# JS divergence on one core: four fp32 first loads made by both hardware queues in halves, with new ranges and orders

## Chip, cores and metric

The kernel runs on one core of a Trainium2 chip. The metric is the device time of one execution in microseconds (us).

## The reference

```python
batch, dim = 1024, 4096            # p, q: fp32, rows sum to 1
def reference(p, q):
    m = 0.5 * (p + q)
    kl_pm = np.sum(p * np.log(p / (m + 1e-8) + 1e-8), axis=-1)
    kl_qm = np.sum(q * np.log(q / (m + 1e-8) + 1e-8), axis=-1)
    return (0.5 * (kl_pm + kl_qm)).astype(np.float32)
```

Each output is a sum over one row of 4096 columns.

## The kernel before

The 1024 rows are 8 row groups (g0 to g7) of 128 rows, one row per partition. Each group is cut along its columns into ranges, and there are four different cuts: `LOADS` (what one load brings), `LOGS` (what one logarithm of p and q covers), `PRODUCTS` (the buffers `ab` that hold these logarithms) and `SUMS` (the ranges of s = p + q and of its logarithm c). Ranges are numbered through all groups. Every quantity is a logarithm with an added constant in place of a quotient: with a = ln(p), b = ln(q) and c = ln((p + q) / 2), all three scaled alike by `SHIFT`, a row's result is 0.5 times the sum of p(a - c) + q(b - c).

The first two ranges (`HW = 2`) are loaded as fp32 into buffers of their own: p by the queue of SyncE (SP), q by that of ScalarE (ACT). All other ranges are loaded by GpSimd (POOL), which issues a load for p and one for q per range (L178, L179); these loads cast to fp16 on the way. The fp16 data of all groups have room of their own and are not overwritten by later loads.

The operations have a letter and a number, and the order on each engine is written out by hand:

- `a` (VectorE): s = p + q for the two fp32 ranges. `F` (TensorE): s = p + q for all others, by matmuls with the identity into PSUM (L264); two PSUM buffers take turns, so F(j) waits until s(j-2) has been used up.
- `p`, `q` (ScalarE): logarithms of p and of q (L280). For the first `SPLIT` log ranges they are two instructions; from there on one instruction `q` does both.
- `c` (ScalarE): logarithm of s (L298), into one of `C_BUFS` buffers.
- `u`, `x` (VectorE), for groups below `APART`: ab - c (L310), and then times p and q (L320). `X` (TensorE) adds up these products in PSUM by matmuls with half the identity (L359).
- `m`, `s` (VectorE), for groups from `APART` on: the products p a and q b (L327), and s c (L338), each added up by `M` and `S` on TensorE. The last `FUSED_M` m's and `FUSED_S` s's add up on VectorE itself (L331, L342).
- `f` (VectorE): a group's partial sum in PSUM is reduced to one column (L381, L384). For g7 `A` (ScalarE, L370) reduces the PSUM part and `f7` (L375) adds the rest.
- `W` (TensorE): idle matmuls (L252).

ScalarE's queue begins with its two load issues, then comes a load of the activation table and a one-element logarithm (L174), then `p0`. A program builds the instructions in the three written orders, each engine in its own sequence; waits between engines follow from the data and the buffers. The fp32 result is stored by SP at the end.

Of the kernel before, what the change touches and what calls it, by code (L numbers as in the profile page):

```python
# [11 lines left out]
MMN = 512  # L12
SW = (1536, 1536)
AW = 256
AB_BUFS = 4
C_BUFS = 5

LOADS = [  # L20
    [416, 448, 992, 1024, 1216],
    [1280, 1536, 1280],
    [1280, 1280, 1536],
    [1024, 1024, 1024, 1024],
    [1664, 1152, 1280],
    [1664, 1152, 1280],
    [2048, 2048],
    [2048, 2048],
]
LOGS = [  # L30
    [416, 448, 992, 1024, 1216],
    [1280, 1536, 1280],
    [1152, 1408, 1536],
    [2048, 2048],
    [1408, 1408, 1280],
    [2048, 2048],
    [1408, 1536, 1152],
    [1152, 1024, 512, 512, 256, 256, 128, 256],
]
PRODUCTS = [  # L40
    [416, 448, 2016, 1216],
    [1280, 1536, 1280],
    [1152, 1408, 1536],
    [2048, 2048],
    [1408, 1408, 1280],
    [2048, 2048],
    [1408, 1536, 1152],
    [1152, 1024, 512, 512, 256, 256, 128, 256],
]
SUMS = [  # L50
    [416, 448, 768, 224, 1024, 448, 768],
    [1280, 1536, 1280],
    [1152, 1408, 1536],
    [1024, 1024, 1024, 1024],
    [1408, 1408, 1280],
    [1536, 1280, 1280],
    [1024, 1536, 1536],
    [1536, 1536, 1024],
]
HW = 2  # L60
SPLIT = 7

APART = 5
FUSED_M = 1
FUSED_S = 5

# [2 lines left out]


ACT_ORDER = """
p0 q0 c0 p1 q1 c1 p2 q2 c2 c3 p3 q3 c4 p4 q4 c5 c6 p5 q5 c7 p6 q6 c8 q7 c9 q8 c10 q9 c11
q10 c12 c13 q11 c14 c15 q12 c16 q13 c17 c18 q14 c19 q15 c20 q16 c21 c22 q17 c23 q18 c24
q19 c25 q20 c26 q21 c27 q22 c28 q23 q24 q25 q26 q27 q28 A7
"""
PE_ORDER = """
W22 F2 F3 X0 X1 F4 X2 X3 F5 F6 X4 F7 X5 X6 F8 X7 F9 W8 F10 X8 F11 X9 X10 F12 F13 X11 F14
F15 X12 F16 X13 X14 F17 F18 X15 X16 F19 X17 F20 X18 F21 S20 F22 X19 M15 F23 S21 S22 F24  # L80
M16 F25 M17 F26 M18 F27 M19 S23 F28 M20 W10 M21 W4 M22 M23 M24 M25 M26
"""
DVE_ORDER = """
a0 a1 u0 u1 x0 x1 u2 u3 x2 x3 u4 x4 u5 u6 x5 x6 u7 x7 f0 u8 x8 u9 x9 u10 x10 f1 u11 x11
u12 x12 u13 u14 x13 x14 f2 u15 u16 x15 x16 u17 x17 f3 u18 x18 u19 s20 x19 m15 s21 s22 f4
m16 s23 m17 s24 f5 m18 s25 m19 s26 m20 s27 m21 s28 m22 m23 m24 m25 m26 m27 f6 f7
"""


# [1 line left out]
def kernel(  # L91
# [6 lines left out]
    nc = tc.nc  # L98
    P = nc.NUM_PARTITIONS
# [13 lines left out]
    pv = p.rearrange("(p g) d -> g p d", g=n_rg)  # L113
    qv = q.rearrange("(p g) d -> g p d", g=n_rg)
# [21 lines left out]
    def apart(r):  # L136
        return r[0] >= APART

    small = ctx.enter_context(tc.tile_pool(name="small", bufs=1))
    lnp = ctx.enter_context(tc.tile_pool(name="lnp", bufs=AB_BUFS))  # L140
    mid = ctx.enter_context(tc.tile_pool(name="mid", bufs=C_BUFS))
    psp = [
# [7 lines left out]
    early = []  # L150
# [16 lines left out]

    for i in range(HW):
        g, c0, w = loads[i]
        nc.sync.dma_start(out=early[i][:, 0, :], in_=pv[g, :, c0 : c0 + w])  # L170
        nc.scalar.dma_start(out=early[i][:, 1, :], in_=qv[g, :, c0 : c0 + w])
    warm = small.tile([P, 1], fp32, tag="warm")
    nc.vector.memset(warm, 1.0)
    nc.scalar.activation(out=warm, in_=warm, func=Act.Ln)  # L174
    def cast_loads(some):
# [15 lines left out]
        out=half, in0=ident, scalar1=0.5, scalar2=0.0, op0=Alu.mult, op1=Alu.add  # L191
# [3 lines left out]
        out=less, in0=ident, scalar1=-0.5, scalar2=0.0, op0=Alu.mult, op1=Alu.add  # L195
# [9 lines left out]
    def fused(kind, i):  # L205
        return i >= NM - FUSED_M if kind == "m" else kind == "s" and i >= NS - FUSED_S

# [65 lines left out]
    def logs_of_loads(i, which):  # L273
        g, c0, w = logs[i]
        (k,) = [k for k in range(NM) if overlap(prods[k], logs[i])]
        if k not in ab:
            ab_t = lnp.tile([P, 2, prods[k][2]], fp16, tag="ab")
            ab[k] = ab_t
        o = c0 - prods[k][1]
        nc.scalar.activation(  # L280
            out=ab[k][:, which, o : o + w],
            in_=pq(g, c0, w)[:, which, :],
            func=Act.Ln,
            bias=TINY,
            scale=SHIFT,
        )

    def op_p(i):
        assert i < SPLIT
        logs_of_loads(i, 0)  # L290

    def op_q(i):
        logs_of_loads(i, 1 if i < SPLIT else slice(0, 2))

# [95 lines left out]
    def c_free(j):  # L390
        if not apart(parts[j]):
            return ("u", j)
        return ("s", j) if fused("s", j) else ("S", j)

    def ab_free(k):
        if apart(prods[k]):
            return [("m", k) if fused("m", k) else ("M", k)]
        return [("x", j) for j in range(NS) if overlap(prods[k], parts[j])]

    def product_of(i):  # L400
        (k,) = [k for k in range(NM) if overlap(prods[k], logs[i])]
        return k

    def after(kind, i):
        if kind == "F" and i - 2 >= HW:
            return [("s" if apart(parts[i - 2]) else "c", i - 2)]
        if kind == "q" and i < SPLIT:
            return [("p", i)]
        if kind in "pq" and product_of(i) >= AB_BUFS:
            return ab_free(product_of(i) - AB_BUFS)  # L410
        if kind == "c":
            return [("a" if i < HW else "F", i)] + ([c_free(i - C_BUFS)] if i >= C_BUFS else [])
        if kind == "x":
# [24 lines left out]
    while any(queues):  # L438
        moved = False
        for todo in queues:  # L440
            while todo and all(d in emitted for d in after(*todo[0])):
                kind, i = todo.pop(0)
# [18 lines left out]
    want |= {(k.upper(), i) for k, i in want if k in "xms" and not fused(k, i)}  # L461
    want |= {("f", g) for g in range(n_rg)} | {("p", i) for i in range(SPLIT)}
    if act_folds:
# [36 lines left out]
```

## Time and profile before

| | |
|---|---|
| median of 3 runs | 98.97 us (98.71 to 99.11) |
| profiled execution | 98.97 us, span in the profile 96.8 us |
| busy share of the span | ScalarE 93%, VectorE 84%, TensorE 72%, GpSimd 26% |
| granted TensorE clock | 0.992 of full speed |
| read from HBM | 33.55 MB, 347 GB/s over the span |
| GpSimd's loads | 46, 87.7% of the time of 16 DMA engines |
| hardware queues' packets | 720, 2.7% of that time |

The span runs from the first to the last recorded instruction of the core. In the profile's rows the first number of a timeline row is the start in us, the second the time it covers, and the bracket at the end is the idle time of the engine just before it and what ended that. A row can merge several instructions (x2, x5). In the slices of the page each digit is one fortieth of the span, in tenths busy.

### The profile page before, as it was taken

Reading aid. Unit: us, or ns where it says so; the run is one execution under the profiler, and the core shown is the slowest. Engines: PE = TensorE matmul, PEld = TensorE weight load, DVE = VectorE, ACT = ScalarE, POOL = GpSimd, SP = SyncE. Lnnn points to the kernel's source line nnn. Section 1 sums busy time; section 2 is a strip of 40 time slices with the busy share of each in tenths; the row PEclk is TensorE's granted clock in tenths of the full one; section 3 lists DMA queues with packets and bytes.
Section 4 is the critical chain, followed back from the end, with each engine's and each line's share of the span. In section 5 each row is a group of like instructions: output and inputs, shape, how many; then the busy total and the mean of one; then the engine's idle time right before and its main releaser. Section 6 shows DMA issues by size and latency. Waiting matters only on the chain.

```text
span 96.8 us, 1276 instructions
## 1 busy us (share of the span) xinstructions
PE 69.5 (72%) x464; PEld 44.9 (46%) x464; DVE 81.1 (84%) x84; ACT 89.8 (93%) x69; POOL 25.1 (26%) x52
## 2 busy tenths in 40 slices
PE   0797586865895787675769767796974969499840
PEld 0574154524562635251626444465743646177630
DVE  1378879777999877969899999989989879989980
ACT  3789999999998999999999999999997999999960
POOL 5954442423324244342243224330000000000000
PEclk9999999999999999999999999999999999999996
DMA  2999999999999999999999999999999999100000
GB/s 58 346 183 195 208 211 212 213 209 207 221 204 213 209 207 212 206 216 214 210 210 214 213 206 212 215 214 215 217 213 210 215 215 193 25 0 0 0 0 2
DMA packets 7349, 17.29 MB, mean 179 GB/s; under 512 B 944, under 2 KB 1712, under 8 KB 7344
## 3 DMA queue, kind: packets, MB, share of 16 engines
q0 software_dynamic: 6624, 16.34, 87.7%
q1 hardware_dynamic: 432, 0.45, 1.4%
q10 hardware_dynamic: 288, 0.44, 1.3%
q8 instruction: 3, 0.05, 0.2%
q14 instruction: 2, 0.02, 0.0%
HBM read 33.55 MB, written 0.00 MB: 347 GB/s over the span
## 4 chain that ended last, share of the span: by engine, by line
DMA 73%; ACT 9%; issue 8%; DVE 6%; POOL 0%; PE 0%; DVEq 0%; POOLq 0%
DMA t<-in_q_dram 73%; ACT ab_t L280 6%; DVE ab_t L327 3%; ACT c_t L298 3%; DVE c_t L342 1%; DVE ab_t L331 1%; POOL t L178 0%; PE st L264 0%; DVEq L495 0%; DVE run L342 0%; DVE res L375 0%; DVE junk L384 0%; POOLq L484 0%; DVE run L331 0%
## 5 line engine op out<-in xcount | busy, mean ns | idle before, releaser
L280 ACT ACTIVATE ab_t<-t 128x1024 f16<-128x1024 f16 (+14 forms) x36 | 61.1, 1726 | 1.7 <-DMA t<-in_p_dram 1.0
L264 PE MATMUL st<-t,ident 128*128 128x512 f16 (+3 forms) x136 | 33.3, 360 | 11.4 <-DMA t<-in_q_dram 10.7
L359 PEld LDWEIGHTS <-half 128*128 128x128 f16 x264 | 25.3, 97 | 18.5 <-issue 13.7
L298 ACT ACTIVATE c_t<-st 128x1024 f16<-128x1024 f32 (+7 forms) x27 | 30.6, 1158 | 0.5 <-PE st L264 0.5
L310 DVE TENSOR_TENSOR ab_t<-ab_t,c_t 128x2048 f16<-128x2048 f16 (+8 forms) x20 | 24.2, 1223 | 6.5 <-ACT c_t L298 5.0
L359 PE MATMUL acc_t<-t,half 128*128 128x256 f16 (+2 forms) x158 | 19.4, 269 | 6.9 <-DVE t L320 6.8
L264 PEld LDWEIGHTS <-ident 128*128 128x128 f16 x136 | 12.7, 97 | 23.9 <-issue 13.8
L320 DVE TENSOR_TENSOR t<-t,ab_t 128x2048 f16<-128x2048 f16 (+7 forms) x18 | 22.9, 1291 | 0.7
L178 POOL DMA_DIRECT2D t<-in_p_dram x23 | 12.4, 537 | 20.7 <-DMA t<-in_p_dram 19.9
L179 POOL DMA_DIRECT2D t<-in_q_dram x23 | 12.2, 532 | 18.7 <-DMA t<-in_q_dram 18.7
L327 DVE TENSOR_TENSOR ab_t<-t,ab_t 128x4096 f16<-128x4096 f16 (+7 forms) x12 | 14.1, 1202 | 1.4 <-ACT ab_t L280 1.4
L359 PE MATMUL acc_t<-ab_t,half 128*128 128x256 f16 (+1 forms) x106 | 12.7, 267 | 1.5 <-DVE ab_t L327 1.5
L252 PE MATMUL acc_t<-ones,ident 128*128 128x256 f16 x22 | 4.2, 379 | 3.1 <-POOL ident masks.py:199 3.1
L338 DVE TENSOR_TENSOR c_t<-st,c_t 128x1280 f16<-128x1280 f32 (+2 forms) x4 | 5.8, 1483 | 0.0
L342 DVE CUSTOM_DVE_ANT_0 c_t<-st,c_t,run 128x1536 f16<-128x1536 f32 (+1 forms) x3 | 4.9, 1637 | 0.0
L252 PEld LDWEIGHTS <-ident 128*128 128x128 f16 x22 | 2.9, 137 | 4.1 <-POOL ident masks.py:199 3.1
L342 DVE CUSTOM_DVE_ANT_0 c_t<-st,c_t 128x1536 f16<-128x1536 f32 x2 | 3.5, 1757 | 0.3 <-ACT c_t L298 0.3
L359 PE MATMUL acc_t<-c_t,less 128*128 128x256 f16 x20 | 2.7, 272 | 0.8 <-DVE c_t L338 0.8
L252 PE MATMUL acc_t<-ones,zero 128*128 128x256 f16 x22 | 2.9, 272 | 0.0
L174 ACT ACT_TABLE_LOAD x1 | 1.3, 1283 | 1.7 <-PEq L484 1.7
L359 PEld LDWEIGHTS <-less 128*128 128x128 f16 x20 | 1.9, 98 | 1.4 <-issue 1.0
L381 DVE TENSOR_REDUCE res<-acc_t 128x1 f32<-128x256 f32 x6 | 2.5, 417 | 0.0
(24 smaller groups left out, 10.9 us busy)
## 6 DMA issues: line engine op xcount, KB each, us to landing
t<-in_p_dram POOLq DMA_DIRECT2D x4, 512.0 KB, 15.8
t<-in_q_dram POOLq DMA_DIRECT2D x4, 512.0 KB, 16.9
t<-in_p_dram POOLq DMA_DIRECT2D x6, 320.0 KB, 12.4
t<-in_q_dram POOLq DMA_DIRECT2D x6, 320.0 KB, 12.7
t<-in_p_dram POOLq DMA_DIRECT2D x5, 256.0 KB, 11.3
t<-in_q_dram POOLq DMA_DIRECT2D x5, 256.0 KB, 11.0
t<-in_p_dram POOLq DMA_DIRECT2D x2, 416.0 KB, 11.7
t<-in_q_dram POOLq DMA_DIRECT2D x2, 416.0 KB, 12.4
```

What stands on the lines that cost most here:

```text
L178: nc.gpsimd.dma_start(out=v[:, 0, :], in_=pv[g, :, c0 : c0 + w])
L179: nc.gpsimd.dma_start(out=v[:, 1, :], in_=qv[g, :, c0 : c0 + w])
L252: nc.tensor.matmul(out=acc[g][:, :AW], lhsT=weights, rhs=ones, start=alone, stop=alone)
L264: nc.tensor.matmul(out=st[:, b : b + m], lhsT=ident, rhs=v[:, t, b : b + m], start=t == 0, stop=t == 1,)
L280: nc.scalar.activation(out=ab[k][:, which, o : o + w], in_=pq(g, c0, w)[:, which, :], func=Act.Ln, bias=TINY, scale=SHIFT,)
L298: nc.scalar.activation(out=c_t[:, :w], in_=s[j], func=Act.Ln, bias=SHIFT * 1e-8, scale=SHIFT * 0.5)
L310: nc.vector.tensor_tensor(out=v, in0=v, in1=c[j].unsqueeze(1).to_broadcast([P, 2, parts[j][2]]), op=Alu.subtract,)
L320: nc.vector.tensor_tensor(out=into, in0=u, in1=v, op=Alu.mult)
L327: nc.vector.tensor_tensor(out=ab[k], in0=u, in1=ab[k], op=Alu.mult)
L338: nc.vector.tensor_tensor(out=c[j], in0=s[j], in1=c[j], op=Alu.mult)
L342: nc.vector.tensor_tensor_reduce(out=c[j], in0=s[j], in1=c[j], scale=-0.5, scalar=before, op0=Alu.mult, op1=Alu.add, accum_out=now,)
L359: nc.tensor.matmul(out=acc[g][:, :m], lhsT=less if kind == "S" else half, rhs=v[:, t, b : b + m], start=(kind, i) == adds[g][0] and n == 0 ...
```

## The change

Four things change together. The fp32 loads of the first two ranges are each cut into the lower and upper 64 partitions; SP's queue issues the lower half and ACT's queue the upper, for p0, q0, p1, q1 in this order. All four cuts into ranges are new; the fp32 ranges are 512 and 256 columns wide (416 and 448 before). `AB_BUFS` goes from 4 to 5 and `C_BUFS` from 5 to 4, `SPLIT` from 7 to 5, `APART` from 5 to 6, so group 5 goes from m and s to u and x, and `FUSED_S` from 5 to 4. The three orders are written anew for the new ranges.

```diff
-AB_BUFS = 4
-C_BUFS = 5
+AB_BUFS = 5
+C_BUFS = 4
 LOADS = [
-    [416, 448, 992, 1024, 1216],
+    [512, 256, 832, 960, 768, 768],
+    [512, 896, 832, 768, 1088],
+    [1280, 1408, 1408],
+    [1152, 1408, 1536],
     [1280, 1536, 1280],
-    [1280, 1280, 1536],
-    [1024, 1024, 1024, 1024],
-    [1664, 1152, 1280],
-    [1664, 1152, 1280],
-    [2048, 2048],
+    [1408, 1408, 1280],
+    [256, 1536, 1536, 768],
     [2048, 2048],
 ]
 LOGS = [
-    [416, 448, 992, 1024, 1216],
+    [512, 256, 832, 960, 768, 768],
+    [512, 896, 832, 768, 1088],
+    [1280, 1408, 1408],
+    [1152, 1408, 1536],
     [1280, 1536, 1280],
-    [1152, 1408, 1536],
-    [2048, 2048],
     [1408, 1408, 1280],
-    [2048, 2048],
-    [1408, 1536, 1152],
-    [1152, 1024, 512, 512, 256, 256, 128, 256],
+    [256, 1536, 1536, 768],
+    [768, 1024, 896, 512, 512, 384],
 ]
 PRODUCTS = [
-    [416, 448, 2016, 1216],
+    [512, 256, 832, 1728, 768],
+    [512, 896, 832, 1856],
+    [1280, 1408, 1408],
+    [1152, 1408, 1536],
     [1280, 1536, 1280],
-    [1152, 1408, 1536],
-    [2048, 2048],
     [1408, 1408, 1280],
-    [2048, 2048],
-    [1408, 1536, 1152],
-    [1152, 1024, 512, 512, 256, 256, 128, 256],
+    [1792, 1536, 768],
+    [768, 1024, 896, 512, 512, 384],
 ]
 SUMS = [
-    [416, 448, 768, 224, 1024, 448, 768],
+    [512, 256, 448, 384, 384, 384, 960, 768],
+    [512, 896, 832, 768, 1088],
+    [1280, 1408, 1408],
+    [1152, 1408, 1536],
     [1280, 1536, 1280],
-    [1152, 1408, 1536],
-    [1024, 1024, 1024, 1024],
     [1408, 1408, 1280],
-    [1536, 1280, 1280],
-    [1024, 1536, 1536],
-    [1536, 1536, 1024],
+    [256, 1536, 1280, 1024],
+    [1536, 1408, 1152],
 ]
-SPLIT = 7
-APART = 5
+SPLIT = 5
+APART = 6
 FUSED_M = 1
-FUSED_S = 5
+FUSED_S = 4
 ACT_ORDER = """
...
+p0 q0 c0 p1 q1 c1 p2 q2 c2 c3 p3 q3 c4 c5 p4 q4 c6 q5 c7 q6 c8 q7 c9 q8 c10 q9 c11 q10 c12
+q11 c13 q12 c14 q13 c15 q14 c16 q15 c17 q16 c18 c19 q17 q18 c20 c21 q19 c22 q20 c23 q21
+c24 c25 q22 c26 q23 q24 c27 q25 c28 q26 c29 q27 q28 c30 q29 c31 q30 q31 q32 A7
 """
 PE_ORDER = """
...
+W22 F2 F3 X0 X1 F4 F5 X2 X3 F6 X4 X5 F7 F8 X6 F9 X7 F10 X8 F11 X9 F12 X10 X11 F13 W8 X12
+F14 F15 X13 F16 X14 F17 X15 F18 X16 F19 X17 F20 X18 F21 X19 F22 X20 F23 X21 F24 F25 X22
+F26 S25 X23 F27 F28 S26 X24 M21 F29 S27 M22 M23 F30 F31 M24 M25 W10 M26 W4 M27 M28
 """
 DVE_ORDER = """
...
+a0 a1 u0 x0 u1 x1 u2 u3 x2 x3 u4 u5 x4 x5 u6 x6 u7 x7 u8 x8 f0 u9 x9 u10 x10 u11 x11 u12
+x12 u13 f1 x13 u14 x14 u15 x15 u16 x16 f2 u17 x17 u18 x18 u19 x19 f3 u20 x20 u21 x21 u22
+f4 x22 u23 s25 x23 u24 s26 x24 m21 s27 f5 m22 s28 m23 s29 m24 f6 m25 s30 m26 s31 m27 m28
+m29 f7
 """
     for i in range(HW):
         g, c0, w = loads[i]
-        nc.sync.dma_start(out=early[i][:, 0, :], in_=pv[g, :, c0 : c0 + w])
-        nc.scalar.dma_start(out=early[i][:, 1, :], in_=qv[g, :, c0 : c0 + w])
+        for t, v in ((0, pv), (1, qv)):
+            for h, queue in ((0, nc.sync), (P // 2, nc.scalar)):
+                queue.dma_start(
+                    out=early[i][h : h + P // 2, t, :], in_=v[g, h : h + P // 2, c0 : c0 + w]
+                )
```

More of the change, by code (lines that the diff above doesn't have):

```diff
@@ L54 @@
-    [1024, 1024, 1024, 1024],
     [1408, 1408, 1280],
-    [1536, 1280, 1280],
-    [1024, 1536, 1536],
-    [1536, 1536, 1024],
+    [256, 1536, 1280, 1024],
+    [1536, 1408, 1152],
 ]
 HW = 2
-SPLIT = 7
-APART = 5
+SPLIT = 5
+APART = 6
 FUSED_M = 1
-FUSED_S = 5
+FUSED_S = 4
 ACT_ORDER = """
-p0 q0 c0 p1 q1 c1 p2 q2 c2 c3 p3 q3 c4 p4 q4 c5 c6 p5 q5 c7 p6 q6 c8 q7 c9 q8 c10 q9 c11
-q10 c12 c13 q11 c14 c15 q12 c16 q13 c17 c18 q14 c19 q15 c20 q16 c21 c22 q17 c23 q18 c24
-q19 c25 q20 c26 q21 c27 q22 c28 q23 q24 q25 q26 q27 q28 A7
+p0 q0 c0 p1 q1 c1 p2 q2 c2 c3 p3 q3 c4 c5 p4 q4 c6 q5 c7 q6 c8 q7 c9 q8 c10 q9 c11 q10 c12
@@ L77 @@
+q11 c13 q12 c14 q13 c15 q14 c16 q15 c17 q16 c18 c19 q17 q18 c20 c21 q19 c22 q20 c23 q21
+c24 c25 q22 c26 q23 q24 c27 q25 c28 q26 c29 q27 q28 c30 q29 c31 q30 q31 q32 A7
 """
 PE_ORDER = """
-W22 F2 F3 X0 X1 F4 X2 X3 F5 F6 X4 F7 X5 X6 F8 X7 F9 W8 F10 X8 F11 X9 X10 F12 F13 X11 F14
-F15 X12 F16 X13 X14 F17 F18 X15 X16 F19 X17 F20 X18 F21 S20 F22 X19 M15 F23 S21 S22 F24
-M16 F25 M17 F26 M18 F27 M19 S23 F28 M20 W10 M21 W4 M22 M23 M24 M25 M26
+W22 F2 F3 X0 X1 F4 F5 X2 X3 F6 X4 X5 F7 F8 X6 F9 X7 F10 X8 F11 X9 F12 X10 X11 F13 W8 X12
@@ L82 @@
+F14 F15 X13 F16 X14 F17 X15 F18 X16 F19 X17 F20 X18 F21 X19 F22 X20 F23 X21 F24 F25 X22
+F26 S25 X23 F27 F28 S26 X24 M21 F29 S27 M22 M23 F30 F31 M24 M25 W10 M26 W4 M27 M28
 """
 DVE_ORDER = """
-a0 a1 u0 u1 x0 x1 u2 u3 x2 x3 u4 x4 u5 u6 x5 x6 u7 x7 f0 u8 x8 u9 x9 u10 x10 f1 u11 x11
-u12 x12 u13 u14 x13 x14 f2 u15 u16 x15 x16 u17 x17 f3 u18 x18 u19 s20 x19 m15 s21 s22 f4
-m16 s23 m17 s24 f5 m18 s25 m19 s26 m20 s27 m21 s28 m22 m23 m24 m25 m26 m27 f6 f7
+a0 a1 u0 x0 u1 x1 u2 u3 x2 x3 u4 u5 x4 x5 u6 x6 u7 x7 u8 x8 f0 u9 x9 u10 x10 u11 x11 u12
```

## The prediction

> **What bounds the kernel now.** I read first the page's busy table: ScalarE (ACT) works 93% of the span, VectorE (DVE) 84%, TensorE 72%.
>
> ```profile
> PE 69.5 (72%) x464; PEld 44.9 (46%) x464; DVE 81.1 (84%) x84; ACT 89.8 (93%) x69; POOL 25.1 (26%) x52
> ...
> DMA  2999999999999999999999999999999999100000
> ```
>
> The slices say that the DMA engines are as full as ACT, but only until slice 34, 84 us. Behind both is one speed each. The loads come at 1.21 ns per column of p or of q (GpSimd's issue of a later load waits for the landing of an earlier one, and these issues are 1.24 us apart for 1024 columns, 1.84 for 1536). A column pair thus takes 2.42 us per 1000 to land, and ACT takes three logarithms of it, 2.50 us per 1000 plus a fixed part per instruction. ACT is the slower by a little, so it should wait only where loads and order don't fit. The timeline of ACT shows where it does:
>
> ```profile
> 1.66 1.28 ACT L174 ACT_TABLE_LOAD   x1 [1.66 <-PEq L484]
> ...
> 3.79 0.99 ACT L280 ACTIVATE ab_t<-t 128x416 f16<-128x416 f32 x2 [0.64 <-DMA t<-in_p_dram]
> ...
> 7.01 1.03 ACT L280 ACTIVATE ab_t<-t 128x992 f16<-128x992 f16 x1 [0.39 <-DMA t<-in_p_dram]
> 8.20 1.03 ACT L280 ACTIVATE ab_t<-t 128x992 f16<-128x992 f16 x1 [0.17 <-DMA t<-in_q_dram]
> ...
> 30.55 2.55 ACT L280 ACTIVATE ab_t<-t 128x2816 f16<-128x2816 f16 x1 [0.31 <-DVE t L320]
> ...
> 74.28 1.45 ACT L298 ACTIVATE c_t<-st 128x1536 f16<-128x1536 f32 x1 [0.49 <-PE st L264]
> ...
> 92.60 0.63 ACT L280 ACTIVATE ab_t<-t 128x512 f16<-128x512 f16 x1 [0.19 <-DVE ab_t L327]
> ```
>
> After p0 starts at 3.79, ACT idles 0.39 + 0.17 + 0.31 + 0.49 + 0.19 = 1.55 us before A7 starts at 93.17. The rest, 93.17 - 3.79 - 1.55 = 87.83 us, is work. The 0.49 at 74.28 is put down to PE, but PE itself was late for the last q piece of a 2048-wide load:
>
> ```profile
> 73.87 0.38 PE L264 MATMUL st<-t,ident 128*128 128x512 f16 x1 [1.88 <-DMA t<-in_q_dram]
> ```
>
> That is why the chain of waits is mostly DMA up to 74 us, and ACT and DVE from there. What remains is the tail on VectorE, 93.23 (end of the last log) to 94.50:
>
> ```profile
> 93.26 0.75 DVE L331 CUSTOM_DVE_ANT_0 ab_t<-t,ab_t,run 128x512 f16<-128x512 f16 x1 [0.47 <-ACT ab_t L280]
> ...
> 93.94 0.48 DVE L384 CUSTOM_DVE_ANT_0 junk<-acc_t,ones,run 128x256 f16<-128x256 f32 x1
> 94.35 0.08 DVE L384 DVE_READ_ACCUMULATOR2_ANT res<- 128x1 f32 x1
> 94.35 0.15 DVE L375 TENSOR_TENSOR res<-folded,run 128x1 f32<-128x1 f32 x1
> ```
>
> The page ends at 96.8, 2.3 us after this; the profiled execution took 98.97, 2.17 more, and that is the median of the three runs as well. I keep 2.3 + 2.17 unchanged.
>
> **What the Trainium skill says.** "DMA: Bandwidth & Descriptors", Rules for kernel authors, on two transfers to disjoint partition halves: both halves spray over the same 16 engines and serialize, so halving brings no bandwidth. The trace agrees in kind: in 2.4 to 4.8 us two hardware queues and the software queue together wrote 347 GB/s, and the engines were full. What can change is the order, p before q. "ScalarE: Activation LUTs", What ACT_TABLE_LOAD costs: about 1283 ns; the trace has 1283. The same section has back-to-back activations overlapping by some 93 ns after 186 ns of fixed time, so 93 ns net; here the log of 4096 elements (3632 ns) starts 3.52 us ahead of its successor, 0.107 over 4096 x 0.8333 ns. I use 0.10 per log and 0.055 per c (1024 columns from PSUM: 0.91 against 0.853).
>
> **The change, part by part.**
>
> *Start.* Each queue now issues four loads, not two. On ACT an issue takes 0.40 to 0.46 us and the table load stands behind the issues: they ran 0.74 to 1.63, the load began at 1.66. Two more move it to 1.66 + 0.86 = 2.52, its end to 3.80, and with the warm-up's 0.20 p0 to about 4.03, **0.24 later**. If an issue of 64 rows were cheaper, p0 could come with its data, and this would be a gain: before, 832 columns had landed at about 3.85 and 1728 at 5.15, 1.45 ns each, so the first 512 are there at 3.4, q0 (1024 in all) at 4.1, p1 and q1 at 4.5 and 4.9. Taken: +0.24, bounds -0.4 and +0.6. a0 (128 x 448 took 0.63, so about 0.69 for 512) can run 4.15 to 4.84, and c0 wants it at 5.1: the later q is hidden by the logs of p0 and q0. From p0 to the point where p2 was wanted ACT took 6.62 - 3.79 = 2.83; 96 columns fewer (96 x 3 x 0.833 = 0.24) make it 2.59, so ACT asks for p2 at 6.6. p2's landing at 7.0 followed 2720 columns; now it follows 2368, 352 x 1.21 = 0.43 sooner, 6.57. p2 (832: 0.79) ends at 7.4, q2 lands at 7.58: idle 0.2, where before there were 0.56.
>
> *Logs.* The elements are the same, 98,304 per row. Separate p and q logs go from 7 ranges to 5, but the ranges from 29 to 33: 38 logs for 36. The c's go from 29 to 32. 2 x 0.10 + 3 x 0.055 = **+0.37** of ACT work.
>
> *Loads against logs.* 27 casting pairs for 23, all still at 1.21 to 1.25 ns a column in the widths the trace has (992 to 2048; no fixed part is visible), so the last q still lands at 84.1. I added the durations along the new order and set the landings beside them. After q2 each load lands ahead of its log or c: by 0.1 us at q3, 0.2 at q12, elsewhere by 0.3 or more, from q14 (38 us) on by 0.7 or more; c24 to c27 (66 to 76 us) have 1.5 and more. The 0.49 at 74.28 goes, since g6 is now loaded in four pieces. Last is c30, whose F30 has its last piece at 84.15 + 0.8 = 85.0 and which ACT reaches at 85.4 to 86. ab has five buffers for four, so the two waits for VectorE (0.31, 0.19) should go; c has four for five, but c(j) needs only that u(j-4) is done, two logs earlier. I leave 0.1. GpSimd issues 54 loads for 46 at 0.53 us: it had 39 us of waiting and hides that. Idle on ACT: 0.2 + 0.1 for 1.55, **-1.25**.
>
> *Tail.* f6 moves ahead of m25, so its 0.41 leaves the end; but the last product is 384 wide, not 256: its fused form on 768 elements lies between 0.75 (512) and 1.28 (1024, from PSUM), about 1.0, 0.25 more. M28 has four matmuls that A7 waits for (eight took 1.03, four some 0.6), which puts f7 about level with m29. Tail 1.25 to 1.35 for 1.27: **0**.
>
> *VectorE and PE.* Group 5 goes from m and s to u and x, 25 + 25 for 20 + 20 operations: with the durations by width the sum of all grows by 0.5 us, beside ACT. From u24 on (q22 ends at about 70.8) I add u24 1.49, s26 1.75, x24 1.49, m21 2.02, s27 1.48, f5 0.42, m22 1.76, s28 1.28, m23 0.95, s29 1.80, m24 0.95, f6 0.42, m25 1.22, s30 1.66, m26 1.09, s31 1.40, m27 and m28 0.69 each, m29 1.0: 23.6, less 18 overlaps of 0.08: 22.2, so 93.0. ACT's last log ends at about 92.6 and m29 after it at 93.63: VectorE has 0.6 us to spare, no more. PE: F has 144 matmuls for 136, the other sums 280 for 284: even, with 28% idle.
>
> **Sum**: 0.24 + 0.37 - 1.25 + 0 = -0.64, so 98.97 - 0.64 = **98.3 us**.
>
> **Rivals.** *Same time* (98.5 to 99.4): the halves land late, and the DMA stream with them. For: the skill promises nothing from halves, and neither 64-row loads nor casting loads under 992 columns occur in the trace. At 0.05 us more for each of the eight added loads and 0.3 at the start, 0.7 us are lost: 99.0. Against: 128-row pieces show no fixed part.
>
> *Slower* (99.6 to 100.4): **VectorE becomes the bound in the last 25 us.** u and x of one range now mostly follow each other directly; a dependent pair leaves a gap of 0.08 (u ends 14.25, x starts 14.33) where independent ones overlap by 0.08, and there are 17 such pairs for 9: 8 x 0.16 = 1.3, with the 0.5 above 1.8. If that lateness is not absorbed by u24, m29 ends at 93.0 + 1.8 = 94.8 or later, and with ACT then held up by PSUM and c buffers that wait for s26 to s29 another 0.5 to 1: 99.3 to 100.4. The point from which it counts is a u24 later than 71.4; it ends slower by 0.5 when u24 is 1.9 us late. For: only 0.6 to spare. Against: VectorE idled 2.2 us of the last 30 before, and per 1408 columns it needs 3.3 us where ACT takes 3.7.
>
> *Larger gain* (97.3 to 97.9): 64-row issues at half price, p0 at 3.5, no wait left: 0.6 more.
>
> **How the numbers follow.** Forecast 0.45, same 0.25, VectorE 0.20, larger gain 0.10. Half a per cent, 0.5 us, is about what a measurement of this kernel can tell from no change; the forecast's own range, 97.9 to 98.8, straddles its bound at 98.48, with two thirds below. Faster: 0.45 x 0.7 + 0.10 + some of the rest = 0.46; slower 0.23; same 0.31. The range, 97.5 to 99.7, leaves out the far end of each outer case.
>
> **What would show it.** ACT's table load at about 2.5 and p0 at 4.0; p2 at 6.6; no ACT wait for PE near 74 us; last log near 92.6; m29 straight after it. Wrong if p0 comes at 3.5 or after 4.5, if ACT waits for VectorE or PE by over 0.5 us in sum, or if VectorE runs without a gap from 71 us and m29 starts over 0.3 us after the last log.

## The result, and the profile after

The changed kernel took 102.04 us (median of 6 executions), the kernel before 98.85 us (6 executions): ratio 1.0312, 95% interval 1.0269 to 1.0354. Ratios here and below are taken over the executions within 1.5% of the fastest of the same kernel, so that they can differ a little from the ratio of the medians. It is 3% slower, where 98.3 us and a range up to 99.7 were forecast. Its profiled execution took 101.75 us with a span of 100.0.

The page of the changed kernel, busy time and DMA slices:

```profile
PE 68.5 (68%) x468; PEld 45.5 (45%) x468; DVE 81.6 (82%) x87; ACT 89.9 (90%) x74; POOL 29.3 (29%) x60
...
DMA  1999999999999999999999999999999993000000
```

ACT works as long as before, 89.9 us for 89.8, in a span that is 3.2 us longer. So about 3.2 us of idle time are new on it. The timeline of the changed kernel, ACT with its queue, has most of them at the start (1.1 us ahead of p0 and 1.3 behind it; of the rest, most lies behind the last result, see "Why the prediction was wrong"):

```profile
0.74 0.57 ACTq L174 DMA_DIRECT2D t<-in_p_dram  x1
1.33 0.86 ACTq L174 DMA_DIRECT2D t<-in_q_dram  x1
2.22 0.62 ACTq L174 DMA_DIRECT2D t<-in_p_dram  x1
2.87 0.62 ACTq L174 DMA_DIRECT2D t<-in_q_dram  x1
3.52 1.28 ACT L179 ACT_TABLE_LOAD   x1 [3.52 <-issue]
...
4.92 0.61 ACT L285 ACTIVATE ab_t<-t 128x512 f16<-128x512 f32 x1
6.15 0.63 ACT L285 ACTIVATE ab_t<-t 128x512 f16<-128x512 f32 x1 [0.62 <-DMA t<-in_q_dram]
7.05 0.63 ACT L303 ACTIVATE c_t<-s 128x512 f16<-128x512 f32 x1 [0.27 <-DVE s L244]
7.59 0.40 ACT L285 ACTIVATE ab_t<-t 128x256 f16<-128x256 f32 x1
9.49 0.42 ACT L285 ACTIVATE ab_t<-t 128x256 f16<-128x256 f32 x1 [1.50 <-DMA t<-in_q_dram]
10.12 0.42 ACT L303 ACTIVATE c_t<-s 128x256 f16<-128x256 f32 x1 [0.21 <-DVE s L244]
10.44 1.67 ACT L285 ACTIVATE ab_t<-t 128x832 f16<-128x832 f16 x2
```

p0 starts at 4.92 (before: 3.79), and then ACT waits 0.62 for q0 and 1.50 for q1, and 0.27 and 0.21 for the sums that need them. p2 starts at 10.44; before it was 7.01, and 6.6 was predicted. From there to the end there are two waits: 0.23 us at 17.17, and one in the tail:

```profile
92.87 2.94 ACT L285 ACTIVATE ab_t<-t 128x1024 f16<-128x1024 f16 x3
96.54 0.38 ACT L375 ACTIVATE unused<-acc_t 128x256 f16<-128x256 f32 x1 [0.73 <-PE acc_t L364]
```

The waits near 30, 74 and 92 us that the kernel before had are gone, as predicted. VectorE's tail (same kernel):

```profile
95.84 1.02 DVE L336 CUSTOM_DVE_ANT_0 ab_t<-t,ab_t,run 128x768 f16<-128x768 f16 x1
...
97.05 0.16 DVE L380 TENSOR_TENSOR res<-folded,run 128x1 f32<-128x1 f32 x1 [0.18 <-ACT unused L375]
```

So the new ranges do what was expected of them, and the loads lose several times as much, most of it ahead of p2. Where the data were is seen in the view of the loads, from issue to landing in us:

```profile
t<-in_p_dram ACTq DMA_DIRECT2D x1, 128.0 KB, 3.2
t<-in_p_dram SPq DMA_DIRECT2D x1, 128.0 KB, 2.7
t<-in_q_dram ACTq DMA_DIRECT2D x1, 128.0 KB, 4.8
t<-in_q_dram SPq DMA_DIRECT2D x1, 128.0 KB, 4.6
...
t<-in_p_dram SPq DMA_DIRECT2D x1, 64.0 KB, 5.0
t<-in_p_dram ACTq DMA_DIRECT2D x1, 64.0 KB, 5.3
t<-in_q_dram SPq DMA_DIRECT2D x1, 64.0 KB, 5.9
t<-in_q_dram ACTq DMA_DIRECT2D x1, 64.0 KB, 6.6
```

The later a half is issued, the longer it takes to land, although the halves of p1 and q1 are the smallest loads of the kernel: ACT's half of q1, issued at 2.87, lands 6.6 us later.

### The profile page after: what moved, and what is told of

Read it like the earlier page. It is cut to its first block, busy times and chain, and to the rows that moved or that the text cites. A ratio compares the mean times of both kernels' runs of the same rounds, so it can differ in the third digit from the quotient of the medians.

```text
span 100.0 us, 1324 instructions
## 1 busy us (share of the span) xinstructions
PE 68.5 (68%) x468; PEld 45.5 (45%) x468; DVE 81.6 (82%) x87; ACT 89.9 (90%) x74; POOL 29.3 (29%) x60
## 4 chain that ended last, share of the span: by engine, by line
ACT 47%; issue 22%; DVE 3%; PE 1%; ACTq 0%
ACT ab_t L285 24%; ACT c_t L303 23%; DVE c_t L347 1%; PE acc_t L364 1%; DVE t L325 1%; DVE ab_t L332 1%; ACT unused L375 0%; DVE res L386 0%; ACTq L303 0%; DVE res L380 0%; ACTq L500 0%; ACTq L285 0%; DVE run L347 0%
## 5 line engine op out<-in xcount | busy, mean ns | idle before, releaser
L285 ACT ACTIVATE ab_t<-t 128x2816 f16<-128x2816 f16 (+15 forms) x38 | 63.6, 1718 | 2.1 <-DMA t<-in_q_dram 2.1
L364 PEld LDWEIGHTS <-half 128*128 128x128 f16 x268 | 25.6, 99 | 33.2 <-issue 24.5
L364 PE MATMUL acc_t<-t,half 128*128 128x256 f16 (+2 forms) x200 | 24.4, 270 | 16.7 <-DVE t L325 16.6
L315 DVE TENSOR_TENSOR ab_t<-ab_t,c_t 128x2816 f16<-128x2816 f16 (+12 forms) x25 | 29.3, 1179 | 5.8 <-ACT c_t L303 4.9
L303 ACT ACTIVATE c_t<-st 128x1408 f16<-128x1408 f32 (+13 forms) x30 | 33.2, 1135 | 0.2 <-PE st L269 0.2
L269 PE MATMUL st<-t,ident 128*128 128x512 f16 (+4 forms) x144 | 31.8, 357 | 1.0 <-DVE c_t L343 0.8
L325 DVE TENSOR_TENSOR t<-t,ab_t 128x2816 f16<-128x2816 f16 (+11 forms) x23 | 28.2, 1233 | 1.2
L364 PE MATMUL acc_t<-ab_t,half 128*128 128x256 f16 x68 | 9.2, 274 | 7.4 <-DVE ab_t L325 4.4
L332 DVE TENSOR_TENSOR ab_t<-t,ab_t 128x1536 f16<-128x1536 f16 (+5 forms) x8 | 9.3, 1172 | 0.1
L343 DVE TENSOR_TENSOR c_t<-st,c_t 128x256 f16<-128x256 f32 (+2 forms) x3 | 3.6, 1217 | 0.0
L347 DVE CUSTOM_DVE_ANT_0 c_t<-st,c_t,run 128x1408 f16<-128x1408 f32 (+1 forms) x2 | 3.1, 1549 | 0.0
## 6 DMA issues: line engine op xcount, KB each, us to landing
t<-in_q_dram POOLq DMA_DIRECT2D x4, 320.0 KB, 12.8
```

Source lines behind the costliest of these rows:

```text
L269: nc.tensor.matmul(out=st[:, b : b + m], lhsT=ident, rhs=v[:, t, b : b + m], start=t == 0, stop=t == 1,)
L285: nc.scalar.activation(out=ab[k][:, which, o : o + w], in_=pq(g, c0, w)[:, which, :], func=Act.Ln, bias=TINY, scale=SHIFT,)
L303: nc.scalar.activation(out=c_t[:, :w], in_=s[j], func=Act.Ln, bias=SHIFT * 1e-8, scale=SHIFT * 0.5)
L315: nc.vector.tensor_tensor(out=v, in0=v, in1=c[j].unsqueeze(1).to_broadcast([P, 2, parts[j][2]]), op=Alu.subtract,)
L325: nc.vector.tensor_tensor(out=into, in0=u, in1=v, op=Alu.mult)
L332: nc.vector.tensor_tensor(out=ab[k], in0=u, in1=ab[k], op=Alu.mult)
```

## Experiments

The first four separate the parts of the change and the parts of the loss.

**1. The ranges alone.** Everything of the change but the halves:

```diff
-        for t, v in ((0, pv), (1, qv)):
-            for h, queue in ((0, nc.sync), (P // 2, nc.scalar)):
-                queue.dma_start(
-                    out=early[i][h : h + P // 2, t, :], in_=v[g, h : h + P // 2, c0 : c0 + w]
-                )
+        nc.sync.dma_start(out=early[i][:, 0, :], in_=pv[g, :, c0 : c0 + w])
+        nc.scalar.dma_start(out=early[i][:, 1, :], in_=qv[g, :, c0 : c0 + w])
```

> New ranges and orders, but each fp32 load whole again: p by SP, q by ACT (two issues on each queue). Theory A (the halved loads cost all of the loss, the ranges and orders save 0.6 us): q1 lands by 5.2 us, no wait of ACT over 0.5 us before 12 us, 98.2 us, ratio 0.990 to 0.997 to before. Rival B (the ranges and orders lose by themselves, VectorE being the bound at the end): 100 us or more, ratio 1.012 or more, and VectorE without a gap from 71 us on.

Measured: 97.89 us, ratio 0.9924 (0.9910 to 0.9938): a gain of 0.8%, faster than both kernels. ACT's timeline of this kernel:

```profile
1.65 1.28 ACT L175 ACT_TABLE_LOAD   x1 [1.65 <-PEq L485]
...
4.49 1.15 ACT L281 ACTIVATE ab_t<-t 128x512 f16<-128x512 f32 x2 [1.34 <-DMA t<-in_p_dram]
5.55 0.61 ACT L299 ACTIVATE c_t<-s 128x512 f16<-128x512 f32 x1
6.07 0.71 ACT L281 ACTIVATE ab_t<-t 128x256 f16<-128x256 f32 x2
6.68 0.40 ACT L299 ACTIVATE c_t<-s 128x256 f16<-128x256 f32 x1
6.98 1.67 ACT L281 ACTIVATE ab_t<-t 128x832 f16<-128x832 f16 x2
```

ACT waits once, 1.34 us for p0, and then not until 27.74 (0.20). The tail of the same kernel shows that VectorE was near its bound, as the slower rival had it, without being pushed over it:

```profile
92.52 1.02 DVE L332 CUSTOM_DVE_ANT_0 ab_t<-t,ab_t,run 128x768 f16<-128x768 f16 x1
...
93.72 0.16 DVE L376 TENSOR_TENSOR res<-folded,run 128x1 f32<-128x1 f32 x1 [0.18 <-ACT unused L371]
```

The last log ends at 92.48 and m29 starts at 92.52. From 70.97 on, VectorE has had no gap beyond 0.2 us. Theory A stands, but for the 1.34 us that ACT waits for p0, which it had not; B falls.

**2. The halves alone**, in the kernel before (the diff of 1 the other way round).

> Ranges and orders of before, with only the four fp32 loads halved over both queues. Theory A: the same late q1 as in the changed kernel (landing at 9 us or later, against 5.2), 3 us or more lost at the start, 102 to 102.6 us. Rival B: at most 0.5 us of it, 99 to 99.5 us.

Measured: 103.53 us, ratio 1.0476 (1.0425 to 1.0526): worse than expected, 4.8% where the halves cost 3.9 points in the new ranges (1.0312 against 0.9924). ACT starts p2 at 10.97, 4.0 us later than in the kernel before. With the new ranges alone faster than before (run 1), the whole loss comes with the halves.

**3. The casting loads 1.4 us later.** GpSimd is made to wait, by two memsets:

```diff
+    late = small.tile([P, 1024], fp32, tag="late")
+    for _ in range(2):
+        nc.gpsimd.memset(late, 0.0)
     cast_loads(loads[HW : HW + 1])
```

> The changed kernel with two memsets of 128x1024 fp32 on GpSimd (about 2 us) ahead of its first casting load, so that GpSimd's loads come to the DMA engines when the halves are through. Theory A1 (the halves are late because they take turns with casting loads that are already queued): q0 lands by 4.3 and q1 by 5.5 us; ACT starts p0 at 4.9 as before, since it still issues four loads, and then has no wait over 0.3 us up to p2; 99.5 to 100.3 us. Theory A2 (64-row loads are slow in themselves): q1 lands at 9 us still, and the time is 101.5 us or more.

Measured: 100.05 us, ratio 1.0154 (1.0112 to 1.0196). The time is A1's, the landings are so in part: q0 came at 5.1, not by 4.3, but ACT waited for it no more (0.62 before), p1 at 5.4, and q1 at 8.5 still. The first casting load was issued from 2.64 to 3.30, ahead of the end of the last half's issue (2.86 to 3.48), and its first packets were in the DMA engines at 4.3: p0, q0 and p1 came through, q1 did not. q0 and p1, of 64 rows too, took 3.2 to 3.8 us from issue to landing, against 4.6 to 5.3 in the changed kernel, which speaks against A2; q1 left it open.

**4. The table load ahead of ACT's four issues** (the warm-up's memset and logarithm are moved ahead of the loop of loads).

> The changed kernel with the table load and the warm-up logarithm ahead of ACT's four load issues. Theory A (late p1 and q1 set the pace, the table load behind the issues costs nothing on its own): p0 starts at 3.5 to 4.1 in place of 4.9, q1's log still waits until 9.5 or later, and the time stays within 0.5 us of the changed kernel's 101.8. Rival C (the issues ahead of the table load are the cost): 1.1 us less, 100.6.

Measured: 101.05 us, ratio 1.0222 (1.0193 to 1.0252): 0.9 points less than the changed kernel, between A and C. p0 started at 4.35, since its data were later than before (the table load ended at 2.01), q0 waited 1.47, q1 0.65, and p2 started at 9.79. Of the 3.9 points that the halves cost, moving the table load ahead of the issues gives back 0.9: those issues are the smaller part of the loss.

**5. The casting loads 4.4 us later**: as 3, with five memsets.

> The changed kernel with five of the memsets (about 5 us) ahead of GpSimd's first casting load; looked at for the landings alone, its time is spoilt by late casting loads. Theory A1 (halves wait for casting loads that are in the engines at the same time): with none there before 7 us, q1 has landed by 6 us, 3.4 us or less after its issue, in place of 8.5 to 9.4. Theory A2 (the 64-row loads are slow in themselves): q1 lands at 8 us or later.

Measured: 102.6 us in a single execution, as expected spoilt by late loads (and by VectorE, which waited for the identity that GpSimd made late). The landings are what it was for:

```profile
t<-in_q_dram SPq DMA_DIRECT2D x1, 128.0 KB, 3.7
t<-in_q_dram ACTq DMA_DIRECT2D x1, 128.0 KB, 3.9
...
t<-in_q_dram SPq DMA_DIRECT2D x1, 64.0 KB, 3.2
t<-in_q_dram ACTq DMA_DIRECT2D x1, 64.0 KB, 3.1
```

q1 lands 3.1 us after its issue, in place of 6.6, at 6.0. The halves of 64 rows are not slow to land in themselves; what makes them so is GpSimd's loads beside them. A1 stands.

**6. Halves of the columns**: the same eight loads with 128 rows each.

```diff
-            for h, queue in ((0, nc.sync), (P // 2, nc.scalar)):
+            for h, queue in ((0, nc.sync), (w // 2, nc.scalar)):
                 queue.dma_start(
-                    out=early[i][h : h + P // 2, t, :], in_=v[g, h : h + P // 2, c0 : c0 + w]
+                    out=early[i][:, t, h : h + w // 2], in_=v[g, :, c0 + h : c0 + h + w // 2]
                 )
```

> The changed kernel with each fp32 load cut into two halves of the columns (128 rows each), in place of the rows: the same number of issues on the same queues and the same bytes. If the number of loads is the matter (each more load a further turn behind a casting load, and two more issues ahead of the table load): q1 at 9 us or later, 101.5 to 102.5 us. If the 64 rows are the matter (longer issues, 0.55 to 0.86 us against 0.38 to 0.46[...]): issues of 0.45 us, q1 by 6.5 us, 99.5 us or less.

Measured: 101.9 us (median of 4, from 100.5 to 102.3), ratio 1.0257 (1.0207 to 1.0307). ACT's timeline of this kernel, in the execution of 100.53:

```profile
1.17 0.46 ACTq L174 DMA_DIRECT2D t<-in_q_dram  x1
...
4.03 1.13 ACT L285 ACTIVATE ab_t<-t 128x512 f16<-128x512 f32 x2
5.22 0.63 ACT L303 ACTIVATE c_t<-s 128x512 f16<-128x512 f32 x1
7.31 0.42 ACT L285 ACTIVATE ab_t<-t 128x256 f16<-128x256 f32 x1 [1.46 <-DMA t<-in_p_dram]
8.44 0.42 ACT L285 ACTIVATE ab_t<-t 128x256 f16<-128x256 f32 x1 [0.72 <-DMA t<-in_q_dram]
```

Both answers are partly right. With 128 rows an issue takes 0.40 to 0.46 us, so p0 starts at 4.03, the very time that the prediction gave for the halves of rows. q0 is there in time, but p1 and q1 are late all the same. So the 64 rows are not needed for late loads, they add the longer issue; whether the number of loads makes them late, or only that p1 and q1 are issued later behind more loads (from 1.63 on, for 1.17 in run 1), is what the next run tells apart.

**7. All four whole loads by SP** (`nc.scalar.dma_start` becomes `nc.sync.dma_start`), so that ACT issues none and p0 is truly ahead.

> New ranges with whole fp32 loads, all four issued by SP in the order p0, q0, p1, q1; ACT issues none, so its table load stands first. Theory B1 (the queues take turns, and from 2.9 us on each hardware load waits for one casting load of 1.0 us): p0 lands at 3.3, q0 at 4 to 5, q1 at 6.5 or later, and ACT waits for them: 98.3 to 99.5 us. Theory B2 (casting loads come in only when a hardware queue runs dry): the four follow each other without a gap, p0 at 3.3, q0 at 4.0, q1 by 5.2: ACT starts 1.1 us earlier than with p and q side by side and ends 0.5 to 0.9 us earlier, 97.0 to 97.4 us.

Measured: 99.98 us, ratio 1.0149 (1.0111 to 1.0187). ACT's timeline and the loads of this kernel:

```profile
3.50 1.23 ACT L281 ACTIVATE ab_t<-t 128x512 f16<-128x512 f32 x2 [1.27 <-DMA t<-in_p_dram]
...
7.73 0.42 ACT L281 ACTIVATE ab_t<-t 128x256 f16<-128x256 f32 x1 [2.20 <-DMA t<-in_p_dram]
9.13 0.42 ACT L281 ACTIVATE ab_t<-t 128x256 f16<-128x256 f32 x1 [0.98 <-DMA t<-in_q_dram]
```

```profile
t<-in_p_dram SPq DMA_DIRECT2D x1, 256.0 KB, 2.7
t<-in_q_dram SPq DMA_DIRECT2D x1, 256.0 KB, 2.9
t<-in_p_dram SPq DMA_DIRECT2D x1, 128.0 KB, 6.1
t<-in_q_dram SPq DMA_DIRECT2D x1, 128.0 KB, 7.0
```

No halves at all, four loads as before the change, and the same picture. p0 and q0, issued by 1.60, land in 2.9 us or less; p1 and q1, issued at 1.65 and 2.11, take 6.1 and 7.0. So it is not the number of loads but when each is issued. B1 had the waits, though its time was too low.

The trace's DMA records, summed by queue over half microseconds, show what goes on (thousands of bytes written; a casting load reads twice what it writes):

```
from (us)                 1.5  2.0  2.5  3.0  3.5  4.0  4.5  5.0  5.5  6.0  6.5  7.0  7.5
whole loads (run 1)   SP   22   63   75   86  105   38    1    0    0    0    0    0    0
                     ACT    2   30   75   94   69  104   16    0    0    0    0    0    0
                   casts    0    0    0    0    0   28   93   94   88  100  107  101  103
changed kernel        SP    0   79   51    4   10   67   47    3   19   68   31    8    2
                     ACT    0    4  104   22    0   12   96   22    1   48   30   34   11
                   casts    0    0    6   59   86   54   28   71   84   37   58   69   96
```

With whole loads the two queues write from 1.5 to 4.5 us without a gap and the casts come in as they end. In the changed kernel, most of p0 is through at 3.0, hardly any of q0 comes before 4.0, and the casts have the time between; from then on everything shares. It is the casts that push q0 back: in run 5, with the same eight issues and no cast before 7.0, SP and ACT wrote 131 and 95 KB from 3.0 to 4.0 us, where they write 14 and 22 here. In run 7, from 4.0 to 8.0 us, the records have 275 packets of SP beside 310 of casts, about one for one, and a casting packet reads 3.3 KB where one of p1 reads 1. That fits what the Trainium skill says in "DMA: Bandwidth & Descriptors", Queues, rings and completion order: each engine goes round the queues that have work, a packet from each. It doesn't explain when the casts come in: with whole loads on two queues they were issued as early and had nothing written before 4.0.

**8 to 10. The casts held back to fit.** Identity first, then one memset (for 7 and for 6) or two (for the changed kernel), and then the first casting load:

```diff
-    cast_loads(loads[HW : HW + 1])
     ident = small.tile([P, P], fp16, tag="ident")
     make_identity(nc, ident)
+    late = small.tile([P, 1024], fp32, tag="late")
+    for _ in range(1):            # 2 in the changed kernel
+        nc.gpsimd.memset(late, 0.0)
+    cast_loads(loads[HW : HW + 1])
```

> All four whole fp32 loads on SP, as before, but GpSimd makes the identity and one memset of 128x1024 (1 us) ahead of its first casting load, whose issue then ends at about 2.9, after SP's last one (2.54). Theory D (a hardware load whose issue ends after that of GpSimd's first casting load shares the engines with the casts and lands 5 to 7 us after its issue; one that is issued ahead of it lands in about 4): p1 and q1 land by 5.3 (in place of 7.7 and 9.1), ACT starts p0 at 3.5 and has no wait over 0.5 us behind it; 97.0 to 97.6 us, ratio 0.983 to 0.990. Rival E (a single queue is too slow, or 2 us of casting loads are missing later): p1 still at 7 or later, 99.5 us or more.

> The changed kernel with the identity and two of the memsets ahead of the first casting load (issue ends at about 3.9; the last half's issue ends at 3.48). Theory D: q0 by 5.2 and q1 by 6.2, ACT starts p0 at 4.9 (four issues ahead of the table load) and waits under 0.4 us in all up to p2: what is left of the loss is the later start, 0.4 us against whole loads: 98.0 to 98.6 us. Rival (halves have a cost of their own beyond that): 99.5 us or more.

> The column halves with the identity and one memset ahead of the first casting load (issue ends at about 2.9, the last half's at 2.6). Theory D: q1 lands by 5.5 in place of 8.4, p0 starts at 4.0, no wait over 0.4 us up to p2: 97.5 to 98.1 us, against 101.9 without the memset. Rival (number of loads): 100 us or more.

Measured: 99.51 (ratio 1.0050, 1.0021 to 1.0079), 100.07 (1.0128, 1.0095 to 1.0161) and 100.04 us (1.0116, 1.0081 to 1.0151). All three are better than without the delay (ratios 1.0149, 1.0312, 1.0257), and all three miss the times of Theory D by 1.5 to 2.5 us and lie where their rivals put them (rival E's late p1 did not come: 6.6, not 7 or later). The landings about held for the row halves (q0 5.2, q1 6.8 for 6.2):

```profile
4.91 1.13 ACT L288 ACTIVATE ab_t<-t 128x512 f16<-128x512 f32 x2
6.15 0.63 ACT L306 ACTIVATE c_t<-s 128x512 f16<-128x512 f32 x1
...
8.24 1.91 ACT L288 ACTIVATE ab_t<-t 128x832 f16<-128x832 f16 x2 [0.34 <-DMA t<-in_p_dram]
```

(ACT, changed kernel with the delay.) The waits for q0 and q1 are gone and one of 0.34 for p2 is there. In the other two, q1 came at 7.2 and 7.5 in place of the 5.3 and 5.5 expected: the issue of the casts ended 0.2 to 0.3 us after the last fp32 load's, yet their packets met the last fp32 packets in the engines (in the SP kernel, casts from 4.1 on, SP's last at 6.9). Theory D, the order of issue alone, is too simple; what overlaps is slowed. And p2 itself now lands later, which I had left out: at 8.7 in the SP kernel. Its log starts at 8.2 to 8.7 in the three, for 6.98 in run 1, and the two with eight loads lose 0.4 us more at the very end.

**11 and 12. Earlier starts with whole loads.** The first two ranges in the order 256, 512, and as 384, 384, in all four cuts:

> New ranges with whole fp32 loads, and the first two ranges exchanged: 256 columns, then 512. p0's landing gates ACT at 4.49 with 512 columns first. With 256 first p0 and q0 should land by 3.5, p1 and q1 at about 5.0: ACT starts p0 at 3.5, waits 0.3 us for p1, and reaches p2 at 6.5 in place of 6.98: 97.4 us, ratio 0.985 to 0.991 to before. If the wait moves to p1 in full, there is no gain: 97.9.

> New ranges with whole fp32 loads, the first two ranges 384 columns each. With 512 first ACT waited for p0 until 4.49, with 256 first it started at 3.28 but waited 0.51 for p1 and 0.70 for p2. If the end follows the start of p2's log (86.2 us from there to A7 in every run so far) and p2 lands at 6.6 as with 512 first: p0 at 3.8, no wait for p1, p2 at 6.6, 97.5 us, ratio 0.986 to 0.990. If p2 lands at 7.2 as with 256 first: 98.1 to 98.4 us.

Measured: 98.34 us (ratio 0.9963, 0.9941 to 0.9986) and 98.1 us (0.9898, 0.9860 to 0.9937). Neither shows a gain over run 1 (0.9924, 0.9910 to 0.9938): the first is behind it, and the interval of the second overlaps with it. With 256 first, p0 starts at 3.28, but p1 is waited for (0.51) and p2 (0.70). With 384 each, p0 at 3.88 and p2 at 6.56 came as expected; but 0.22 us of the 0.42 won on run 1 went with a wait for q2, and its profile, of the slowest of the six executions (98.76), lost the rest at 25.6 us. The same log in run 1, and then in this kernel:

```profile
24.49 2.08 ACT L281 ACTIVATE ab_t<-t 128x2176 f16<-128x2176 f16 x1
```

```profile
25.64 2.02 ACT L281 ACTIVATE ab_t<-t 128x2176 f16<-128x2176 f16 x1 [1.19 <-DMA t<-in_q_dram]
```

This one load of q landed at 25.56, in run 1 at 23.88, with its neighbours within 0.3 us of theirs there; what held it up is open, and whether the other executions had it too is not known. Where ACT starts earlier, the first casting loads (p2 and q2) are the next thing that it waits for.

**All runs on one scale.** Start of p2's log and start of A7 on ACT, us from the span's start, in the profiled execution of each kernel (a single one, up to 1.4 us from the kernel's median):

| kernel (new ranges) | p2 | A7 | between |
|---|---|---|---|
| 384, 384 whole | 6.56 | 93.98 | 87.42 |
| 512, 256 whole (run 1) | 6.98 | 93.21 | 86.23 |
| 256, 512 whole | 7.25 | 93.58 | 86.33 |
| row halves, casts after | 8.24 | 94.31 | 86.07 |
| column halves, casts after | 8.49 | 94.89 | 86.40 |
| SP alone, casts after | 8.73 | 94.76 | 86.03 |
| column halves | 9.39 | 95.33 | 85.94 |
| row halves, casts late | 9.50 | 95.70 | 86.20 |
| row halves, table first | 9.79 | 95.76 | 85.97 |
| row halves, casts 4.4 us later | 9.87 | 97.38 | 87.51 |
| SP alone | 9.98 | 96.07 | 86.09 |
| changed kernel | 10.44 | 96.54 | 86.10 |

Two rows have one long wait of ACT behind p2 that the others have not: 1.19 us in the first (above), and 1.63 where the casts are latest. Without it they come to 86.23 and 85.88, and all twelve are the same to about 0.5 us, whatever was done to the loads: a microsecond of delay ahead of p2 is a microsecond at A7. The time behind A7 falls into two groups: 4.8 us with four fp32 loads, 5.2 with eight.

## Why the prediction was wrong

**The step that failed is "Start".** It gave +0.24 us, with bounds of -0.4 and +0.6. Measured against whole loads in the same ranges, p2 came 3.46 us later (10.44 against 6.98), and A7 3.33. The sum, with the same terms read from the profiled executions (against 98.97 us before):

| term, us | predicted | run 1, whole loads | changed kernel |
|---|---|---|---|
| start of p0 | +0.24 | +0.70 | +1.14 |
| ACT idle from p0 to the last log | -1.25 | -1.34 | +1.27 |
| ACT's work in that stretch | +0.37 | -0.11 | +0.17 |
| last log to the end of f7 | 0 | +0.13 | +0.13 |
| end of f7 to the end of the span | 0 | +0.01 | +0.44 |
| device time outside the span | 0 | -0.36 | -0.37 |
| sum | -0.64 | -0.97 | +2.78 |

Two terms of the step were mis-sized, and the order of the landings was turned over.

- *The issues.* Four of them were to take 4 x 0.43 on ACT. They took from 0.74 to 3.49, 2.75 us, since an issue of 64 rows costs more than one of 128 (0.57 to 0.86 against 0.40 to 0.46), not the same or half. p0 started at 4.92, not 4.03, past the 4.5 that the prediction had named as a sign of being wrong. I had bounded this cost below by half and above by nothing but the 0.6.
- *The landings.* I carried on 1.45 ns per column from the two landings of before, as if only bytes counted. That slope was measured with all four loads issued by 1.63 us, ahead of the casts. Issued up to 3.49, the later ones met the casts: q0 landed at about 6 us, not 4.1; q1 at 9.5, not 4.9. "The later q is hidden by the logs of p0 and q0" thus had no cover, and 2.60 us of waits took its place.
- *p2's landing,* by contrast, was early enough: casts were ahead of q1, so p2's 832 columns were there (PE's first sum of them, F2, began at 6.86) while ACT waited until 9.49 for the 256 of q1:

```profile
6.86 1.15 PE L269 MATMUL st<-t,ident 128*128 128x448 f16 x4
```

A term that the prediction kept "unchanged" failed too, the 2.3 us behind f7: 2.75 to 2.78 with eight fp32 loads, 2.34 to 2.35 with four, in every kernel. The trace's records of SP's semaphore instructions (a semaphore is a counter that tells of landings and of other engines' work) show why. At the end SP checks them one after another, 0.06 us each. In run 1 six of these checks run while the result is on its way out, and one behind its landing; in the changed kernel the result's semaphore comes second, and seven more checks follow its landing at 98.65. It is so in each of the fourteen kernels, by the number of its fp32 loads.

The rival "same time" had the right place ("the halves land late") with 0.3 us for it, a tenth of what it was. The rival on the slower side was put on VectorE. That 0.23 for slower came out is no merit: it rested on another cause.

**What was right.** The waits that the ranges and orders take away: -1.34 us for -1.25 in run 1, with whole loads. ACT's waits behind p2 are 0.20 there in place of 0.99 (0.31, 0.49 and 0.19), where 0.1 was reckoned, and the last log ends at 92.48 for 92.6. c24's wait near 74 us is gone, and no buffer wait of ACT is left. Tail: 1.40 us from the last log to the end of f7 (92.48 to 93.88) for 1.25 to 1.35. A7 waits 0.73 for M28, as VectorE is just in time: m29 started 0.04 after the last log. The estimate of VectorE's last stretch (0.6 to spare) was thus somewhat high, and its lateness, the slower rival's mechanism, cost next to nothing: 0.04 at m29, and at most the 0.18 for which f7 waits for A7.

**What was luck.** Without the start step the sum is 0.37 - 1.25 + 0 = -0.88, and run 1 gained 0.74 us on the medians (98.63 to 97.89). The nearness is in part luck. p0, now 512 columns wide and loaded beside q0, came 0.70 later than before, a loss that the sum has not; ACT's five further logs and c's cost nothing that shows, where 0.37 was set; and 0.34 of the 0.74 lies outside the span (98.63 less 96.5 before, 97.89 less 96.1 in run 1). That part, the "2.17" kept unchanged, is 2.1 to 2.2 us in all executions with the old ranges, halves or not, and 1.7 to 1.9 in all with the new. No run shows what it is made of.

**The Trainium skill's rule** ("DMA: Bandwidth & Descriptors", Rules for kernel authors) against loads of disjoint partition halves was quoted and taken to mean that no bandwidth is gained, a zero. The zero hid a loss: its other side, in the same page's section Issuing engines are not separate DMA queues, is that issuing from several engines only saves issue time. Here, with each load cut in two, it spent issue time: 2.75 us on ACT for 0.88 before, on the queue that holds the table load, and its loads race against a third queue.

**Still open:** what exactly admits the casts. They begin at 2.9 us in the changed kernel and after 4.0 with whole loads on two queues, though GpSimd issues them at 1.24 in both. Mostly, an fp32 load whose issue ended ahead of that of the first casting load landed within 4.1 us, and one whose issue ended later took 4.6 to 7.0. The exceptions are p1 and q1 with one memset (SP alone and column halves, 4.2 to 5.4 us; ahead by 0.7 us for p1, by 0.2 to 0.3 for q1) and SP's half of q1 in run 3 (5.4; ahead by 0.1): late nonetheless. The order of issue isn't all.

## What to carry over

Before a load is cut or moved to another queue, count its issue on the issuing engine and ask what other queue will fill the gap: a few tenths of a microsecond of later issue put the first data behind a stream that was ready and waiting. A landing time measured in one order of issue can't be carried on to another by bytes. Where one engine is busy from its first data to the end, find the instant at which its steady run begins and price each edit by what it does to that instant. And look at what lies behind the last result, too: here the number of loads cost 0.4 us there.

## What the runs showed of the hardware

- The issue of a load on SP or ACT took 0.36 to 0.46 us with 128 rows, at 128 to 512 columns alike, and 0.54 to 0.90 us with 64 rows.
- The last of 27 pairs of casting loads, eleven of them under 1152 columns, landed at 84.17 us in run 1; the last of the 23 pairs before, six of them under 1152, at 84.11.
- In the changed kernel TensorE stood idle for 3.99 us ahead of 12.0, and from 12.8 to 16.2 us it was granted half of its clock. Eight of the fourteen kernels have such a halving, first seen between 7.9 and 12.8 us, and each of these has an idle stretch of TensorE of 1.8 to 4.0 us that ends at most 1.3 us ahead of it or reaches into it; the other six have no halving there, and between their first matmuls and 16 us no idle stretch over 1.0 us. That the one brings about the other was not tested, and idle stretches of 1.8 us near 20 us were followed by none. The page of the changed kernel:

```profile
PEclk9999957999999999999999999999999999999996
```
